# h's parts laid out by pairs of k over four token blocks, in a hybrid attention and MLP block

## The chip, the cores and the metric

The kernel runs on one core of a Trainium2 chip. The metric is the device time of one execution in microseconds. A comparison is made on medians of several runs; the profile beside it is of one execution.

## What is computed

One decoder layer on a sequence of 1024 tokens with a width of 1024, in float32. The part that the change touches is the first third: a normalized and modulated input h, and one projection of it to 2304 columns, from which two kinds of attention take their heads. The rest is the output projection and an MLP of width 4096 with squared ReLU.

```
h = rms_norm(x, g_attn_pre) * (1 + sc_a) + sh_a
proj = h @ w_in                                   # 1024 x 2304
oa = banded_attention(...)                        # window of 128, with sinks
ob = dilated_mixture_attention(...)               # three dilated windows
mixed = concat([rms_norm(oa, g_mix_a), rms_norm(ob, g_mix_b)])
x = x + gt_a * rms_norm(mixed @ w_out, g_attn_post)
h = rms_norm(x, g_mlp_pre) * (1 + sc_m) + sh_m
x = x + gt_m * rms_norm(square(relu(h @ w_up)) @ w_down, g_mlp_post)
```

## The kernel before

**Numbers in two parts.** Every matmul operand is split into an upper part, a float32 rounded to the format that TensorE takes (fp32r), and a lower part, the rest. One product is three matmuls: upper by upper, lower by upper, upper by lower. ACT writes an upper part with a copy, DVE or POOL the lower one with a subtraction.

**Where h lies.** The tile `hw` has 128 partitions, 8 slots, 2 parts and 1024 floats (line 422). Tokens are counted in eight blocks of 128, the width of h in eight pieces k of 128 (the contraction). Before, slot t holds token block t; inside it piece k stands at 128k. `mod_chunk` (lines 677 to 695) fills it from `xnT`, the transposed normalized input: for one k, ACT writes the upper part (line 689), then h itself in place (line 686), and DVE the lower part (line 692). For k 0 and 1 it does so in two halves of four token blocks, for the others over all eight at once.

**The projection.** There are six units u (two of them for the banded attention, four for the dilated one), each of three column tiles c of 128 and two token halves x of 512. A tile (u, x, c) adds eight products, one for each k, in one bank of PSUM. `proj_mm` (lines 859 to 869) emits the three matmuls (lines 866, 867 and 869): the stationary operand is the weight, the moving one is h of the half x, read as four blocks of 128 tokens out of four slots. The first unit goes through `first_unit` (tile name `acc`), the others through `proj_tile` (tile name `pj`), whose products are the "dense" work of PE that stands between the steps of attention.

**The order of the work.** The program is written out by a planner, the class `Sched`. It holds a queue of steps for every engine, each with a planned duration, what it waits for, and resources that it takes and gives (`Res`). It emits whichever step can start first by its own clock, so planned durations and the moments at which resources come free decide the order of the instructions on each engine. Each engine then works through its instructions in that order; real waits are those of the data and of the tiles. A planned release that has no tile behind it is no wait on the chip.

**Where h's place goes next.** `hw` is used again. When the projection is nearly done, `load_wo` (lines 1339 to 1365) brings in `w_out` in eight parts k: a DMA to a staging tile (line 1348), a multiplication by a column of gains on ACT into `hw[:, k, 0]` (line 1353), and the lower part into `hw[:, k, 1]` by DVE (line 1356) or by POOL in two instructions (lines 1361 and 1362), whichever the planner finds free. Each part takes one unit of the resource `r_wo`; it is given by `proj_tile` in the last column tile (u 5, c 2): four units after the last k of x 0, four after the last k of x 1. `load_wo` is opened when at most two projection tiles are still to be emitted. `open_out` (lines 1367 to 1381) opens the output projection when the dense work is done, the last tile of the projection has been handed on, and all eight parts of `w_out` have been planned. It loads a gate (line 1377); then `out_block` takes one token block after another: it loads the attention output (line 1423), splits it (lines 1436 and 1439) and multiplies it with the parts in `hw` (lines 1478 to 1480, tile name `y_ps`).

**Attention.** A step of it has scores on PE (lines 1127 and 1182), a maximum on DVE (1146), exponentials on ACT (1153), the normalization on POOL (1158), transposes on PE (1232 to 1239), the split of the result on ACT and DVE (1246 and 1250) and the product with the values on PE (1262 to 1274).

**The MLP** fills the rest of the time, with seven products of quarters for each of its eight halves (lines 1902 to 1904).

Of the kernel before, what the change touches and what calls it, by code (L numbers as in the profile page):

```python
# [10 lines left out]
F32 = mybir.dt.float32  # L11
# [4 lines left out]
ALU = mybir.AluOpType  # L16
# [3 lines left out]
P = 128  # L20
D = 1024
S = 1024
KC = D // P
# [151 lines left out]
class Sched:  # L175
# [20 lines left out]
    def op(self, eng, dur, emit, deps=(), **kw):  # L196

        o = self.step(dur, emit, deps, **kw)
        o.alts = None
        if isinstance(eng, str):  # L200
            self.queue[eng].append(o)
        else:
            o.alts = dict(zip(eng, zip(dur, emit)))
            for e in eng:
                self.queue[e].append(o)
        return o.ev
# [113 lines left out]
def t_sb(n):  # L320
    return 0.098 + 0.00083 * n
# [6 lines left out]
def t_dv(n):  # L328
    return 0.066 + 0.00104 * n
# [19 lines left out]
def hybrid_block(ctx: ExitStack, tc: tile.TileContext, x, positions, w_ada, b_ada, g_attn_post, w_in, w_out,  # L349
# [3 lines left out]
    V, A, G, T = nc.vector, nc.scalar, nc.gpsimd, nc.tensor  # L353
    x, out = x[0], out[0]
    w_ada, w_out, w_up, w_down = w_ada[0], w_out[0], w_up[0], w_down[0]
    sc = Sched()
    op, pe_op = sc.op, sc.pe_op

    def pool(name, bufs=1, side="left", space=None, stack=ctx):
        kw = dict(name=name, bufs=bufs, reuse_waits="tile")  # L360
        if space is not None:
            kw["space"] = space
        else:
            kw["side"] = side
        return stack.enter_context(tc.tile_pool(**kw))
# [20 lines left out]
    r_u, r_raw, r_h2, r_wo = Res(0), Res(0), Res(0), Res(0)  # L386
# [35 lines left out]
    hw = pool("hw", 1).tile([P, KC, 2, 1024], F32R, name="hw")  # L422
# [45 lines left out]
    xnT = p0.tile([P, KC, S], F32, name="xnT")  # L468
# [56 lines left out]
    w_raw, w_rawe, w_hl, w_e = {}, {}, {}, {}  # L525
# [45 lines left out]
    e = op("ACT", 0.1, lambda: A.activation(cond[:], c_raw, AF.Exp, scale=-1.0), [e_c], prio=0)  # L571
# [32 lines left out]
    e = op("DVE", 4.2, f_turns, [e_pos, e_c], prio=1)  # L604
# [34 lines left out]
    def mod_group(g):  # L639
# [30 lines left out]
        for half in ((0, 1) if g == 0 else (None,)):  # L670
            for k in range(2 * g, 2 * g + 2):
                mod_chunk(k, eg, half)
# [4 lines left out]
    def mod_chunk(k, eg, half):  # L677
        t0, t1 = (0, TB) if half is None else (4 * half, 4 * half + 4)
        n = (t1 - t0) * P
        ks = slice(k * P, (k + 1) * P)  # L680
        h, hh = xnT[:, k, t0 * P:t1 * P].rearrange("p (b t) -> p b t", t=P), hw[:, t0:t1, 0, ks]
        deps = [eg] + (e_xn[0] + e_xn[1] if half is None else e_xn[half])

        def full(eng):
            if eng is A:
                return lambda: A.activation(h, h, AF.Identity, bias=s_a[:, k:k + 1], scale=g_a[:, k:k + 1])
            return lambda: V.tensor_scalar(h, h, g_a[:, k:k + 1], s_a[:, k:k + 1], ALU.mult, ALU.add)

        eh = op("ACT", t_sb(n) + 2 * AP_COST, lambda: A.activation(hh, h, AF.Identity, bias=s_a[:, k:k + 1],
                                                                  scale=g_a[:, k:k + 1]), deps, prio=0)  # L690
        e = op("ACT", t_sb(n) + 2 * AP_COST, full(A), [eh], prio=0)
        e = op("DVE", t_dv(n), lambda: V.tensor_tensor(hw[:, t0:t1, 1, ks], h, hh.bitcast(F32), ALU.subtract), [e],
               prio=0)
        for x in (0, 1) if half is None else (half,):
            e_hh[k, x], e_hl[k, x] = eh, e
# [39 lines left out]
    qs, ks, vs, e_q, e_k, n_in = {}, {}, {}, {}, {}, {}  # L735
# [117 lines left out]
    def dense(dur, emit, deps, **kw):  # L853
        return pe_op("dense", dur, emit, deps, **kw)

    def w_at(u, c, k):
        return divmod(3 * k + c, 4) if u == 0 else (2 * c + k // 4, k % 4)

    def proj_mm(ps, u, c, k, x, part):
        i, n = w_at(u, c, k)  # L860
        t, w = slice(k * P, (k + 1) * P), w_hl[u, i]
        n = slice(n * P, n * P + P)
        h = [hw[:, 4 * x:4 * x + 4, i, t] for i in range(2)]
        ps = ps[:].rearrange("p (b t) -> p b t", t=P)
        if part != 1:
            T.matmul(ps, w[:, 0, n], h[0], start=(k == 0), stop=False)  # L866
            T.matmul(ps, w[:, 1, n], h[0], start=False, stop=False)  # L867
        if part != 0:
            T.matmul(ps, w[:, 0, n], h[1], start=False, stop=(k == KC - 1))  # L869
# [18 lines left out]
    def first_unit():  # L888
        order = [(k, part, x, c) for x in range(2) for k in range(2) for part in range(2) for c in range(3)]
        order += [(k, part, x, c) for k in range(2, AHEAD) for part in range(2) for x in range(2) for c in range(3)]  # L890
        order += [(k, part, x, c) for x in range(2) for c in range(3) for k in range(AHEAD, KC) for part in range(2)]
        last = {w_at(0, c, k)[0]: i for i, (k, _, _, c) in enumerate(order)}
        accs[FILL] = acc_at[FILL][0].tile([P, 512], F32, name="acc", tag=acc_at[FILL][1])
        acc_at[FILL][2].free.pop()
        for i, (k, part, x, c) in enumerate(order):
            a = 3 * x + c
            pl, tag, r = acc_at[a]
            first = k == 0 and part == 0 and a != FILL

            def emit(k=k, part=part, x=x, c=c, a=a, pl=pl, tag=tag, first=first):  # L900
                if first:
                    accs[a] = pl.tile([P, 512], F32, name="acc", tag=tag)
                fill.open |= a == FILL
                proj_mm(accs[a], 0, c, k, x, part)

            def after(k=k, part=part):
                if part:
                    tick()
                if k == KC - 1:
                    sc.filler = None  # L910
            d = dense(0.454 if part == 0 else 0.227, emit,
                      [w_e[0, w_at(0, c, k)[0]], (e_hl if part else e_hh)[k, x]] + (e_xn[0] + e_xn[1] if a == 5 else []),
                      takes=[(r, 1)] if first else [], after=after, gives=[(r_w, 1)] if last[w_at(0, c, k)[0]] == i else [])
            if k == KC - 1 and part:
                yield (0, x, c, lambda a=a: accs[a], d, r)
# [4 lines left out]
    def proj_tile(u, x, c):  # L920
        b = []
        for k in range(KC):
            def emit(k=k):
                if k == 0:
                    b.append(pj.tile([P, 512], F32, name="pj", tag="pj"))
                proj_mm(b[0], u, c, k, x, None)
            gives = []
            if x and k % 4 == 3:
                gives.append((r_w, 1))
            if u == 5 and c == 2 and k == KC - 1:  # L930
                gives.append((r_wo, 4))
            d = dense(0.681, emit, [w_e[u, w_at(u, c, k)[0]]], takes=[(r_pj, 1)] if k == 0 else [], gives=gives, after=tick)
        evac(u, x, c, lambda: b[0], d, r_pj)

# [11 lines left out]
    def feed_proj():  # L946
        if len(sc.pe.get("dense", [])) <= 4 and todo_dense:
            u, x, c = todo_dense.pop(0)
            if (x, c) == (1, 0):
                next_unit_w(u)  # L950
            if (u, x, c) == (2, 0, 0):
                for e_ in e_tab:
                    e_.clear()
                tables([(0, 1, 4)], lambda i: stage("rows")[:].rearrange("p (b r) -> p b r", b=TB), r_stg, r_x,
                       lambda: px.tile([P, 4, P], F32, name="ptab", tag="x"), [[e_rot[1, 0]], [e_rot[1, 1]]])
            proj_tile(u, x, c)
        return not todo_dense
# [1122 lines left out]
```

## Time and profile before

| | |
|---|---|
| median of 3 runs | 1147.73 us (1147.73 to 1148.61) |
| the profiled execution, its own time | 1148.87 us |
| its span, first to last instruction | 1147.1 us |
| mean granted TensorE clock | 0.992 of full speed |
| projection among attention ends, first output matmul | 377.55 us, 398.38 us from the span's start |
| matmuls | 5417 |

How to read what follows: times in rows are microseconds from the start of the span, unless marked ns. PE is TensorE with its matmuls, PEld its weight loads, DVE is VectorE, ACT is ScalarE, POOL is GpSimd, SP issues the DMAs. A row of the timeline has start, duration, engine, line of the kernel, operation, output and inputs, count, and in brackets the idle time ahead of it with what ended it. A row of the groups has line, engine, operation, shapes and count, then the busy time and the mean duration of one in ns, then idle time ahead. A matmul's recorded duration runs from its entry to the end of its output, so two that follow each other closely overlap in the record.

### The profile page before, as it was taken

What the parts mean: (1) busy time and instruction counts of PE and PEld (TensorE: products, weight loads), DVE (VectorE), ACT (ScalarE), POOL (GpSimd) and SP (SyncE); (2) the same over time, 40 slices, a digit from 0 to 9 for tenths busy, and PEclk for the clock granted to TensorE, in tenths of its full rate; (3) what the DMA queues carried; (4) which work ended last, traced back from release to release, by engine and by line L of the source; (5) the groups of instructions that cost most, each with busy time, mean ns of one, the idle gap of its engine ahead of it and who ended that gap; (6) DMA issues with size and microseconds to landing.
All of it is one profiled execution on the core that took longest, in us unless ns stands there. A gap on an engine that the chain in (4) does not pass through costs nothing.

```text
span 1147.1 us, 15609 instructions
## 1 busy us (share of the span) xinstructions
PE 1115.2 (97%) x5417; PEld 924.1 (81%) x5417; DVE 818.7 (71%) x1380; ACT 635.9 (55%) x1101; POOL 265.7 (23%) x349
## 2 busy tenths in 40 slices
PE   8999999999999899998999999999999999999996
PEld 7788878888888687887788888888888888888885
DVE  7878666666667765668979664599644896537998
ACT  8868865464556756675675424563234733246542
POOL 2458867565743521111000000000000000000002
PEclk9999999999999899998999999999999999999999
DMA  9556454343423305552981168812469112584103
GB/s 347 192 204 164 163 158 164 136 155 127 146 71 132 124 26 186 203 207 104 352 306 39 41 224 285 303 37 74 147 230 332 70 56 76 201 307 168 37 19 147
DMA packets 90910, 185.29 MB, mean 162 GB/s; under 512 B 8400, under 2 KB 31056, under 8 KB 90832
## 3 DMA queue, kind: packets, MB, share of 16 engines
q1 hardware_dynamic: 90832, 184.30, 46.3%
q8 instruction: 43, 0.70, 0.2%
q14 instruction: 35, 0.29, 0.1%
HBM read 137.08 MB, written 28.31 MB: 144 GB/s over the span
## 4 chain that ended last, share of the span: by engine, by line
PE 76%; DVE 8%; issue 4%; ACT 4%; POOL 4%; DMA 3%; SPq 1%; DVEq 0%; POOLq 0%; ACTq 0%
PE mlp_ps L1903 16%; PE mlp_ps L1904 16%; PE mlp_ps L1902 16%; PE pj L866 3%; PE pj L869 3%; PE pj L867 3%; PE s_ps L1127 3%; PE o_ps L1262 2%; PE pt_ps L1232 1%; PE y_ps L1478 1%; PE y_ps L1480 1%; PE y_ps L1479 1%; PE pt_ps L1235 1%; DVE hw L1673 1%; PE o_ps L1267 1%
## 5 line engine op out<-in xcount | busy, mean ns | idle before, releaser
L1902 PE MATMUL mlp_ps<-hw 128*128 128x512 f32 x896 | 350.7, 391 | 0.4 <-ACT hw L1664 0.4
L1903 PE MATMUL mlp_ps<-hw 128*128 128x512 f32 x896 | 349.5, 390 | 1.1 <-DVE hw L1670 1.1
L1904 PE MATMUL mlp_ps<-hw 128*128 128x512 f32 x896 | 349.4, 390 | 0.0
L1903 PEld LDWEIGHTS mlp_ps<-hw 128*128 128x128 f32 x896 | 168.7, 188 | 36.9 <-DVE hw L1670 1.4
L1902 PEld LDWEIGHTS mlp_ps<-hw 128*128 128x128 f32 x896 | 168.8, 188 | 36.4 <-ACT hw L1664 0.8
L1904 PEld LDWEIGHTS mlp_ps<-hw 128*128 128x128 f32 x896 | 168.6, 188 | 35.0
L1673 DVE TENSOR_TENSOR hw<-w,hw 128x1024 fp32r<-128x1024 f32 x96 | 114.7, 1221 | 95.1 <-ACT hw L1666 93.0
L1666 ACT CAST hw<-w 128x1024 fp32r<-128x1024 f32 x96 | 97.5, 1047 | 129.8 <-PE mlp_ps L1904 93.1
L2002 POOL TENSOR_TENSOR st<-st,nhalf 128x1 f32<-128x1 f32 x8 | 7.8, 977 | 604.1 <-DVE st L2000 604.1
L866 PE MATMUL pj<-hw,w_hl 128*128 128x512 f32 x240 | 102.5, 427 | 0.0
L869 PE MATMUL pj<-hw,w_hl 128*128 128x512 f32 x240 | 94.6, 394 | 0.0
L867 PE MATMUL pj<-hw,w_hl 128*128 128x512 f32 x240 | 94.5, 394 | 0.0
L1250 DVE TENSOR_TENSOR ph<-pt_ps,ph 128x512 fp32r<-128x512 f32 (+1 forms) x110 | 69.5, 648 | 34.6 <-ACT ph L1246 34.3
L1666 ACT CAST hw<-u 128x1024 fp32r<-128x1024 f32 x48 | 48.7, 1051 | 64.6 <-PE mlp_ps L1904 64.6
L1246 ACT CAST ph<-pt_ps 128x512 fp32r<-128x512 f32 (+1 forms) x110 | 58.9, 555 | 32.9 <-PE pt_ps L1235 27.5
L1153 ACT ACTIVATE p_sb<-p_sb,mn 128x128 f32<-128x128 f32 (+3 forms) x64 | 49.8, 778 | 38.3 <-DVE mn L1146 36.8
L1673 DVE TENSOR_TENSOR hw<-u,hw 128x1024 fp32r<-128x1024 f32 x48 | 57.1, 1220 | 18.2 <-ACT hw L1666 18.2
L1960 DVE TENSOR_TENSOR yacc<-yacc,mlp_ps 128x512 f32<-128x512 f32 x96 | 62.2, 683 | 3.3 <-PE mlp_ps L1904 3.3
L1158 POOL TENSOR_SCALAR p_sb<-p_sb,den 128x128 f32<-128x128 f32 (+3 forms) x64 | 48.4, 762 | 53.1 <-DVE den L1156 51.9
L1015 POOL TENSOR_TENSOR ada_acc<-ada_acc,wa_st 128x512 f32<-128x512 f32 x42 | 55.3, 1318 | 3.5
L869 PEld LDWEIGHTS pj<-hw,w_hl 128*128 128x128 f32 x240 | 45.1, 188 | 10.5
L1478 PE MATMUL y_ps<-hw,oh 128*128 128x512 f32 x128 | 51.7, 404 | 0.0
(206 smaller groups left out, 2010.4 us busy)
## 6 DMA issues: line engine op xcount, KB each, us to landing
hw<-s_dram SPq DMA_DIRECT2D x84, 512.0 KB, 4.4
wa_st<-in_w_ada SPq DMA_DIRECT2D x32, 512.0 KB, 4.4
w<-in_w_up SPq DMA_DIRECT2D x32, 512.0 KB, 4.8
w<-in_w_down SPq DMA_DIRECT2D x32, 512.0 KB, 7.5
s_dram<-hw SPq DMA_DIRECT2D x28, 512.0 KB, 4.3
qt<-hl SPq DMA_DIRECT2D x40, 256.0 KB, 2.8
w_st<-in_w_in SPq DMA_DIRECT2D x36, 256.0 KB, 3.1
x_sb<-in_x SPq DMA_DIRECT2D x16, 512.0 KB, 6.1
```

The lines of the kernel that those rows point to most:

```text
L866: T.matmul(ps, w[:, 0, n], h[0], start=(k == 0), stop=False)
L867: T.matmul(ps, w[:, 1, n], h[0], start=False, stop=False)
L869: T.matmul(ps, w[:, 0, n], h[1], start=False, stop=(k == KC - 1))
L1246: A.copy(b["ph"][:, 0, :w], b["pt"][:, :w])
L1250: V.tensor_tensor(b["ph"][:, 1, :w], b["pt"][:, :w], b["ph"][:, 0, :w].bitcast(F32), ALU.subtract)
L1478: T.matmul(ps[:], b["oh"][:, k], wh[:, c0:c0 + 512], start=(k == 4 * m), stop=False)
L1666: A.copy(out[j][0], flat(src[j]))
L1673: V.tensor_tensor(out[j][1], flat(src[j]), out[j][0].bitcast(F32), ALU.subtract)
L1902: T.matmul(ps[m][:], sh, mh, start=starts and k == 0, stop=False, **kw)
L1903: T.matmul(ps[m][:], sh, ml_, start=False, stop=False, **kw)
L1904: T.matmul(ps[m][:], sl, mh, start=False, stop=k == 3, **kw)
L1960: e = op("DVE", t_dv(512), lambda: V.tensor_tensor(y(), y(), ps[m][:], ALU.add), [e, ml.e_y[tb, n]], gives=gives, prio=1)
```

## The change

The eight slots of `hw` are numbered anew. Slot 4x + j holds, for the token half x, the pieces k = 2j and 2j + 1, each as one run of 512 tokens. `mod_chunk` writes its two parts there: one run of 512 for a half, two runs for all tokens. `proj_mm` reads one run of 512, and hands PSUM's bank to the matmul without a view in four blocks. Since a slot is now read by two k only, `proj_tile` gives one unit of `r_wo` after each odd k of the last column tile instead of four after the last k. Instructions, their number and their planned durations stay as they are.

```diff
     def mod_chunk(k, eg, half):
         t0, t1 = (0, TB) if half is None else (4 * half, 4 * half + 4)
         n = (t1 - t0) * P
-        ks = slice(k * P, (k + 1) * P)
-        h, hh = xnT[:, k, t0 * P:t1 * P].rearrange("p (b t) -> p b t", t=P), hw[:, t0:t1, 0, ks]
+        h = xnT[:, k, t0 * P:t1 * P].rearrange("p (x t) -> p x t", t=512)
+        hh, hl = (hw[:, t0 // 4 * 4 + k // 2:t1 - 3 + k // 2:4, i, k % 2 * 512:k % 2 * 512 + 512] for i in range(2))
...
-        e = op("DVE", t_dv(n), lambda: V.tensor_tensor(hw[:, t0:t1, 1, ks], h, hh.bitcast(F32), ALU.subtract), [e],
+        e = op("DVE", t_dv(n), lambda: V.tensor_tensor(hl, h, hh.bitcast(F32), ALU.subtract), [e],
                prio=0)
...
     def proj_mm(ps, u, c, k, x, part):
         i, n = w_at(u, c, k)
-        t, w = slice(k * P, (k + 1) * P), w_hl[u, i]
-        n = slice(n * P, n * P + P)
-        h = [hw[:, 4 * x:4 * x + 4, i, t] for i in range(2)]
-        ps = ps[:].rearrange("p (b t) -> p b t", t=P)
+        w, n = w_hl[u, i], slice(n * P, n * P + P)
+        h = [hw[:, 4 * x + k // 2, i, k % 2 * 512:k % 2 * 512 + 512] for i in range(2)]
+        ps = ps[:]
...
-            if u == 5 and c == 2 and k == KC - 1:
-                gives.append((r_wo, 4))
+            if u == 5 and c == 2 and k % 2:
+                gives.append((r_wo, 1))
```

## The prediction

> **What bounds the kernel now.** I read the page's first rows (who is busy), then the table by stage, then the timelines around the one place where the change lets something start earlier.
>
> ```profile
> PE 1115.2 (97%) x5417; PEld 924.1 (81%) x5417; DVE 818.7 (71%) x1380; ACT 635.9 (55%) x1101; POOL 265.7 (23%) x349
> ```
>
> ```profile
> 68.00:377.00 309.00, 304.26 (x1721) 256.03 (x1720) 209.14 (x566) 189.45 (x454) 194.13 (x254) 1.00 0.46 150
> 377.00:398.00 21.00, 15.92 (x92) 12.86 (x91) 17.62 (x48) 17.77 (x35) 12.92 (x11) 0.91 0.32 111
> ```
>
> The second fence is the windows view: window, its length, then busy us of PE, weight loads, DVE, ACT, POOL, then granted clock, DMA share, GB/s. TensorE (PE) is the bound: 304.26 of 309 us while projection and attention share it. Only 377 to 398, after the last projection matmul and before the first of the output projection, has PE at 15.92 of 21: **5.08 us idle**, while DVE (17.62) and ACT (17.77) are nearly full. So the change can pay in two ways: cheaper projection matmuls where PE is full, or a better filled hole at 377.
>
> **The matmuls.** Before, a projection matmul's moving operand is four runs of 128 floats, 8 KB apart; after, one run of 512. The trace of before has both kinds. In the groups by line and shape (count, then busy us, mean ns):
>
> ```profile
> L866 PE MATMUL pj<-hw,w_hl 128*128 128x512 f32 x240 | 102.5, 427 | 0.0
> L867 PE MATMUL pj<-hw,w_hl 128*128 128x512 f32 x240 | 94.5, 394 | 0.0
> L867 PE MATMUL acc<-hw,w_hl 128*128 128x512 f32 x48 | 18.8, 391 | 0.0
> L1479 PE MATMUL y_ps<-hw,oh 128*128 128x512 f32 x128 | 50.4, 394 | 0.0
> L1478 PE MATMUL y_ps<-hw,oh 128*128 128x512 f32 x128 | 51.7, 404 | 0.0
> L1903 PE MATMUL mlp_ps<-hw 128*128 128x512 f32 x896 | 349.5, 390 | 1.1 <-DVE hw L1670 1.1
> ```
>
> L1479, L1478 and L1903 read one run of 512; L866 and L867 read four. L867 takes 394 ns among attention matmuls, exactly what the one-run L1479 takes there, and 391 in the first unit, where little is mixed in, against 390 in the MLP. L866's 427 is that of the first matmul of a group of three, recorded as it enters behind other work (L1478, also first, shows 404 against 394). So the runs cost nothing that these rows show: **0 us** taken. The far end: all 720 `pj` matmuls at the MLP's 390 would be 240 x 37 ns + 480 x 4 ns = 10.8 us less. On the other side even 404 for all gives 720 x 0.404 = 290.9 against 240 x 0.427 + 480 x 0.394 = 291.6: no loss.
>
> **The writes of h.** ACT writes the upper part (L689) and DVE the lower (L692) in eight runs of 128 before, two of 512 after; a half-width call goes from four runs to one.
>
> ```profile
> L689 ACT ACTIVATE hw<-xnT,s_a,g_a 128x1024 fp32r<-128x1024 f32 x6 | 7.1, 1235 | 2.3 <-DVE s_a L668 2.3
> L686 ACT ACTIVATE xnT<-xnT,s_a,g_a 128x1024 f32<-128x1024 f32 x6 | 7.1, 1232 | 0.0
> L692 DVE TENSOR_TENSOR hw<-xnT,hw 128x1024 fp32r<-128x1024 f32 x6 | 7.1, 1221 | 3.0 <-ACT xnT L686 3.0
> L1673 DVE TENSOR_TENSOR hw<-w,hw 128x1024 fp32r<-128x1024 f32 x96 | 114.7, 1221 | 95.1 <-ACT hw L1666 93.0
> ```
>
> L686 does L689's arithmetic into one run: 3 ns less. L1673, the same subtraction in one run, takes 1221 like L692. Ends: 6 x 3 ns gained, nothing lost; taken as 0. Count and planned cost of these instructions stay, so the planner's order stays until the changed `gives` is reached.
>
> **The earlier release.** `hw` is also the place of the output weights: part k of `w_out` goes into slot k. Before, the planner may load parts 0 to 3 after the last k of tile (u 5, x 0, c 2) and parts 4 to 7 after the last k of (5, 1, 2), since every k read every slot of its half. After, slot 4x+k//2 is read by two k alone, and one part is released at each odd k. Nothing is added: no instruction, DMA or wait; eight loads on SP, eight multiplications on ACT and eight lower parts (five on DVE, three as pairs on POOL) move up in their queues. For x 0, PE is full until the projection ends (304.26 of 309 above), so I cost that half at nothing; the cover is the projection, and without it the price would be the 2.18 us that two multiplications hold ACT. For x 1 the L869 of k = 1, 3, 5, 7:
>
> ```profile
> 369.79 0.40 PE L869 MATMUL pj<-hw,w_hl 128*128 128x512 f32 x1
> 372.54 0.39 PE L869 MATMUL pj<-hw,w_hl 128*128 128x512 f32 x1
> 374.83 0.40 PE L869 MATMUL pj<-hw,w_hl 128*128 128x512 f32 x1
> 377.15 0.40 PE L869 MATMUL pj<-hw,w_hl 128*128 128x512 f32 x1
> ```
>
> Four gives at 377.55 become one each at 370.2, 372.9, 375.2 and 377.55: 7.4, 4.6, 2.3 and 0 us earlier, and the later loads no longer queue behind three others. What follows on SP, ACT, DVE and POOL in before:
>
> ```profile
> 372.12 2.03 SPq L1348 DMA_DIRECT2D wo_st<-in_w_out  x4
> ...
> 391.82 0.33 SPq L1377 DMA_DIRECT2D gate_a<-gate_d  x1
> 392.26 0.38 SPq L1423 DMA_DIRECT2D o_sb<-o_dram  x1
> ```
>
> ```profile
> DMA to landing us min/median/max: 4.3/5.1/6.4
> ```
>
> ```profile
> 376.88 0.59 ACT L1246 CAST ph<-pt_ps 128x512 fp32r<-128x512 f32 x1 [2.81 <-PE pt_ps L1235]
> ...
> 384.35 1.16 ACT L1353 ACTIVATE hw<-wo_st,head 128x1024 fp32r<-128x1024 f32 x1
> ...
> 387.82 2.19 ACT L1353 ACTIVATE hw<-wo_st,head 128x1024 fp32r<-128x1024 f32 x2
> ...
> 396.68 1.05 ACT L1436 CAST oh<-o_sb 128x1024 fp32r<-128x1024 f32 x1 [0.73 <-DMA o_sb<-o_dram]
> ```
>
> ```profile
> 384.48 0.69 DVE L847 TENSOR_TENSOR v_hl<-pv,v_hl 128x512 fp32r<-128x512 f32 x1 [0.45 <-ACT v_hl L844]
> ...
> 389.31 2.49 DVE L1356 SCALAR_TENSOR_TENSOR hw<-wo_st,head,hw 128x1024 fp32r<-128x1024 f32 x1
> ```
>
> ```profile
> 380.26 0.59 POOL L1158 TENSOR_SCALAR p_sb<-p_sb,den 128x384 f32<-128x384 f32 x1 [5.79 <-DVE den L1156]
> ...
> 392.86 2.40 POOL L1362 TENSOR_TENSOR hw<-wo_st,hw 128x1024 fp32r<-128x1024 f32 x1
> 395.22 2.47 POOL L1158 TENSOR_SCALAR p_sb<-p_sb,den 128x640 f32<-128x640 f32 x3
> ```
>
> The reader is to see a chain: the last lower part on DVE ends at 391.80; at 391.82 SP issues the gate and then the attention output for block 0 (the output stage opens only when all eight parts are planned); that lands for ACT at 396.68, and PE starts L1478 at 398.38 (last row below). The loads themselves were issued at 372.12 already, since the release is the planner's alone: the chip has the data from about 372.12 + 4.3 = 376.4 on, yet ACT has the multiplications behind attention work until 384.35 to 390.0. After, the first two can run at about 376.5 to 379. That takes two of four, 2.2 us of ACT, out of the stretch where ACT, DVE and POOL hold attention up, and lets POOL (idle 5.79 us before 380.26) do its share before 387 instead of holding the normalizations until 395.22.
>
> ```profile
> 392.78 0.39 PE L1262 MATMUL o_ps<-ph,v_hl 128*128 128x256 f32 x1 [1.33 <-DVE ph L1250]
> ...
> 396.09 0.48 PE L1232 MATMUL pt_ps<-head,p_sb 128*128 128x128 f32 x1 [0.16 <-POOL p_sb L1158]
> 396.97 0.48 PE L1232 MATMUL pt_ps<-head,p_sb 128*128 128x128 f32 x1 [0.40 <-POOL p_sb L1158]
> ...
> 398.38 0.78 PE L1478 MATMUL y_ps<-hw,oh 128*128 128x512 f32 x1
> ```
>
> How early can L1478 come? The next condition is that the last projection is posted, after L847 at 385.17: at most 6.6 us earlier; I take about 4, so near 394.5. An earlier start is worth only the idle PE time it fills: after 394.5 the 0.16 + 0.40 above. The relief of ACT I count at its 2.2 us, PE idling behind those engines. Sum **2.8 us** of the 5.08. The ends: 0, if attention's own chain (PE to ACT to DVE, the 1.33 above) keeps its length, and 5.08, if the hole closes. Past 398 PE is the bound again, so I let the gain last to the end. The profiled execution took 1148.87 (1147.1 of it span), 1.14 above the median of 1147.73, against which the prediction is made: 1147.73 - 2.8 = **1144.9**.
>
> **The rivals.** *The clock keeps up.* Windows of 4 us, same columns:
>
> ```profile
> 380.00:384.00 4.00, 2.79 (x22) 2.23 (x20) 3.38 (x14) 3.88 (x11) 1.65 (x3) 1.00 0.06 16
> 384.00:388.00 4.00, 2.85 (x20) 2.27 (x18) 3.49 (x8) 3.95 (x7) 1.75 (x3) 1.00 0.06 16
> 388.00:392.00 4.00, 2.85 (x19) 2.08 (x17) 4.00 (x7) 3.95 (x7) 3.92 (x3) 1.00 0.09 20
> 392.00:396.00 4.00, 2.93 (x13) 2.37 (x13) 3.33 (x14) 2.53 (x6) 3.92 (x4) 0.80 0.78 250
> 396.00:400.00 4.00, 3.50 (x12) 2.88 (x13) 2.86 (x8) 3.29 (x6) 2.47 (x4) 0.50 0.16 47
> 400.00:404.00 4.00, 4.00 (x27) 3.62 (x26) 2.58 (x6) 1.73 (x3) 0.29 (x2) 0.85 0.00 0
> ```
>
> After 12 us with PE at 71% (8.49 of 12) the granted clock falls to half; 0.20, 0.50 and 0.15 of 4 us each make 3.4 us lost. If PE is fuller before 394, this may not happen: 1144.9 - 3.4 = 1141.5. Against it: the first part of the hole remains, and where the clock decides is not seen. The Trainium skill ("TensorE: Matmul & The Clock Gate", Part 1: The HAM clock gate) has the half rate come back after an idle window of some 3.4 us; by that rule short gaps would not cost the clock, and a fuller PE would change nothing here. The trace disagrees: the longest gap ahead of the fall that the rows show is 1.33 us, and the clock fell.
>
> *Nothing moves.* The matmuls cost the same and attention's own chain sets the hole; 1147.7.
>
> *The four runs do cost.* 427 against 390 is theirs: 1147.73 - 10.8 = 1136.9. L867 at 394 beside the one-run L1479 at 394 speaks against it.
>
> *Slower: a multiplication ahead of its data.* ACT works in order. The planner expects a load within some 3.4 us (its own costs); after the give at 370.2 it may put the first multiplication before the CAST of 376.88. The load issued at 372.12 lands after 5.1 us (median), 6.4 at most: 377.2 to 378.5. Then ACT stands until there, 0.3 to 1.6 us, and so may the next one. The projection that would cover it ends at 377.55, so PE idles as long. Two waits at the far end, 3.2 us: 1150.9. It decides from the point where the first multiplication stands ahead of that CAST and its load lands later than 376.9. For it: the landing times. Against it: ACT idled 2.81 us there anyway.
>
> **How the numbers follow.** Chances: forecast 0.42 (its own range 1142.7 to 1147.7, from 5.08 to 0 gained), clock 0.20, nothing 0.15, four runs 0.04, slower 0.19. A measurement of this kernel tells about 0.2%, 2.3 us, from no change, so faster means below 1145.4. Of the forecast 0.25 lies there; with clock and four runs: faster 0.49. The rest of it, nothing, and a little of slower: same 0.33; slower 0.18. Leaving out the far side of the four runs and the tails of both signs, the range is 1139.5 to 1151.0.
>
> **What would show it.** Right: L867 and L869 stay at 394 and 391; L689 and L692 within 10 ns; the first L1353 of the second half near 377 instead of 384; L1377 and L1478 about 4 us earlier; the stage between last projection and first output matmul with less than 5 us idle; everything up to about 340 us as before. Wrong: matmul means that fall by over 3 ns; L1353 early but PE waiting as long for DVE and POOL; an ACT wait on `wo_st` followed by idle PE; a gain at 398 that is gone by 520.

## The result, and the profile after

The changed kernel is slower: 1150.62 us (median of 17 runs, 1148.62 to 1153.84) against 1147.99 (17 runs, 1146.44 to 1151.07) for the kernel before. The ratio is **1.0025 [1.0017, 1.0032]**, some 2.6 us. (A ratio with an interval is not the quotient of the two medians; it differs from that by up to 0.0007 below.) The forecast was 2.8 us the other way. The execution that was profiled took 1149.36 us, 1.26 below its own median, while that of before lay 0.88 above its median. So the two traces differ by only 0.49 us in total. They show where time moved; how much it is worth is read from the medians.

The line numbers of the kernel after are one lower than those of before from line 863 on: L866, L867 and L869 are now L865, L866 and L868, L1353 and L1356 are L1352 and L1355, L1361 and L1362 are L1360 and L1361, and L1478 is L1477.

First the parts costed at nothing. From the page of after, its busiest engines and two groups:

```profile
PE 1113.5 (97%) x5417; PEld 923.0 (80%) x5417; DVE 821.9 (72%) x1381; ACT 636.0 (55%) x1101; POOL 263.7 (23%) x347
...
L865 PE MATMUL pj<-hw,w_hl 128*128 128x512 f32 x240 | 102.4, 427 | 0.0
L866 PE MATMUL pj<-hw,w_hl 128*128 128x512 f32 x240 | 94.5, 394 | 0.0
```

And from its groups by line and shape, the writes of h:

```profile
L689 ACT ACTIVATE hw<-xnT,s_a,g_a 128x1024 fp32r<-128x1024 f32 x6 | 7.1, 1236 | 2.3 <-DVE s_a L668 2.3
...
L692 DVE TENSOR_TENSOR hw<-xnT,hw 128x1024 fp32r<-128x1024 f32 x6 | 7.1, 1221 | 3.0 <-ACT xnT L686 3.0
```

One run of 512 takes 427 and 394 ns where four runs of 128 took 427 and 394; the writes take 1236 and 1221 against 1235 and 1221. By these rows the layout itself does nothing. The only other difference on the first page is that DVE has one instruction more and POOL two less: one lower part of `w_out` went from POOL to DVE.

The windows of the stage 342 to 378 (start and end, length, then busy us of PE, weight loads, DVE, ACT, POOL, then granted clock, DMA share, GB/s) show a loss where the prediction had counted on a full PE. Before:

```profile
342.00:378.00 36.00, 35.91 (x211) 30.61 (x210) 24.31 (x58) 21.61 (x43) 12.40 (x12) 1.00 0.42 153
```

After:

```profile
342.00:378.00 36.00, 34.30 (x202) 29.11 (x201) 24.77 (x57) 20.68 (x42) 11.52 (x12) 1.00 0.38 138
```

PE loses 1.61 us, with projection products still queued. The timeline of after around 355 says how (start, duration, engine, line, operation, tiles; in brackets the idle time ahead and what ended it):

```profile
352.92 2.40 POOL L1361 TENSOR_TENSOR hw<-wo_st,hw 128x1024 fp32r<-128x1024 f32 x1
...
352.68 0.59 ACT L1245 CAST ph<-pt_ps 128x512 fp32r<-128x512 f32 x1
...
353.22 3.18 DVE L1355 SCALAR_TENSOR_TENSOR hw<-wo_st,head,hw 128x1024 fp32r<-128x1024 f32 x1
356.33 0.68 DVE L1249 TENSOR_TENSOR ph<-pt_ps,ph 128x512 fp32r<-128x512 f32 x1
...
357.06 0.38 PE L1261 MATMUL o_ps<-ph,v_hl 128*128 128x256 f32 x1 [1.40 <-DVE ph L1249]
357.52 0.40 PE L865 MATMUL pj<-hw,w_hl 128*128 128x512 f32 x1
378.79 0.40 PE L868 MATMUL pj<-hw,w_hl 128*128 128x512 f32 x1
```

The reader is to see a chain over four engines. POOL subtracts one lower part of `w_out` from 352.92 to 355.32. DVE starts another at 353.22, which takes 3.18 us and ends at 356.40, 1.08 after POOL's. Behind it in DVE's queue waits attention's split L1249, whose input from ACT was ready at 353.27. It starts at 356.33. The product L1261 waits for it, PE stands for 1.40 us, and the projection products that would fill the gap stand *behind* L1261 in PE's queue. Another 0.30 us of idle PE lies at 348.69 (the row stands below, with e9). The last `pj` matmul starts at 378.79 instead of 377.15. Most of that arises here: from the 636th of the 720 `pj` matmuls, which starts just before 342 in both traces, to the last one it is 36.93 us, against 35.44 before.

In the hole after the projection the same thing comes again, and the chain towards the output stage is longer, not shorter. The matmul L836 that stands 2.28 us here stood 0.41 in before. Timeline of after:

```profile
381.78 2.38 POOL L1361 TENSOR_TENSOR hw<-wo_st,hw 128x1024 fp32r<-128x1024 f32 x1
...
383.27 1.98 DVE L1355 SCALAR_TENSOR_TENSOR hw<-wo_st,head,hw 128x1024 fp32r<-128x1024 f32 x1 [0.56 <-ACT hw L1352]
...
385.63 0.66 PE L836 MATMUL pv<-head,vt 128*128 128x128 f32 x4 [2.28 <-DVE ot L1297]
...
386.20 0.52 SPq L1376 DMA_DIRECT2D gate_a<-gate_d  x1
388.79 3.25 SPq L1300 DMA_DIRECT2D o_dram<-ot  x2
393.57 0.38 SPq L1422 DMA_DIRECT2D o_sb<-o_dram  x1
...
400.76 1.04 ACT L1435 CAST oh<-o_sb 128x1024 fp32r<-128x1024 f32 x1
...
402.80 0.48 PE L1477 MATMUL y_ps<-hw,oh 128*128 128x512 f32 x1
```

The gate L1376 is issued at 386.20, 5.6 us earlier than before. But the attention output of the first block (L1422) comes at 393.57, 1.3 us later than before, behind the stores L1300 of 388.79 on SP's queue. ACT then takes it up only at 400.76, behind attention's work, 7.2 us after its issue where before had it after 4.4. So the first output product comes at 402.80, 4.4 us later.

Why the two profiled executions end nearly together: windows of 4 us near 532, first of before, then of after.

```profile
528.00:532.00 4.00, 0.94 (x5) 0.52 (x4) 2.00 (x2) 1.57 (x3) 2.40 (x1) 0.86 0.00 0
532.00:536.00 4.00, 4.00 (x15) 3.42 (x14) 3.21 (x9) 3.38 (x5) 0.00 (x0) 0.50 0.00 0
536.00:540.00 4.00, 4.00 (x16) 3.21 (x15) 2.75 (x5) 2.10 (x3) 0.00 (x0) 0.78 0.00 0
```

```profile
532.00:536.00 4.00, 2.63 (x11) 2.44 (x12) 1.65 (x6) 3.83 (x5) 0.14 (x1) 0.70 0.00 0
536.00:540.00 4.00, 4.00 (x17) 3.25 (x16) 3.60 (x8) 2.94 (x5) 0.00 (x0) 0.87 0.00 0
```

Before loses 0.14 + 0.50 + 0.22 of 4 us, 3.4 us, after 0.30 + 0.13, 1.7 us. The output products of after end 1.73 us later than those of before (their last one starts at 516.80 against 515.07). From there to the end of the last matmul before takes 622.17 us and after 620.93, so in these two executions the clock gives back most of that. It falls differently from one execution to the next.

### The profile page after: what moved, and what is told of

Read it like the earlier page. It is cut to its first block, busy times and chain, and to the rows that moved or that the text cites. A ratio compares the mean times of both kernels' runs of the same rounds, so it can differ in the third digit from the quotient of the medians.

```text
span 1147.3 us, 15607 instructions
## 1 busy us (share of the span) xinstructions
PE 1113.5 (97%) x5417; PEld 923.0 (80%) x5417; DVE 821.9 (72%) x1381; ACT 636.0 (55%) x1101; POOL 263.7 (23%) x347
## 4 chain that ended last, share of the span: by engine, by line
PE 72%; DVE 9%; DMA 6%; issue 4%; ACT 4%; POOL 4%; SPq 1%; DVEq 0%; POOLq 0%; ACTq 0%
PE mlp_ps L1902 16%; PE mlp_ps L1903 16%; PE mlp_ps L1901 16%; PE pj L865 3%; PE pj L868 3%; PE pj L866 3%; PE s_ps L1126 3%; DMA wa<-in_w_ada 2%; PE o_ps L1261 2%; PE pt_ps L1231 1%; DMA x_sb<-in_x 1%; DVE hw L1672 1%; DMA wo_st<-in_w_out 1%; POOL ada_acc L1014 1%; PE pt_ps L1234 1%
## 5 line engine op out<-in xcount | busy, mean ns | idle before, releaser
L865 PE MATMUL pj<-hw,w_hl 128*128 128x512 f32 x240 | 102.4, 427 | 0.0
L868 PE MATMUL pj<-hw,w_hl 128*128 128x512 f32 x240 | 94.6, 394 | 0.0
L866 PE MATMUL pj<-hw,w_hl 128*128 128x512 f32 x240 | 94.5, 394 | 0.0
L1249 DVE TENSOR_TENSOR ph<-pt_ps,ph 128x512 fp32r<-128x512 f32 (+1 forms) x110 | 69.4, 648 | 26.9 <-ACT ph L1245 26.5
L1672 DVE TENSOR_TENSOR hw<-u,hw 128x1024 fp32r<-128x1024 f32 x48 | 57.1, 1221 | 18.2 <-ACT hw L1665 18.2
L1157 POOL TENSOR_SCALAR p_sb<-p_sb,den 128x128 f32<-128x128 f32 (+3 forms) x64 | 50.9, 799 | 49.7 <-DVE den L1155 44.3
L868 PEld LDWEIGHTS pj<-hw,w_hl 128*128 128x128 f32 x240 | 45.1, 188 | 10.4
L1477 PE MATMUL y_ps<-hw,oh 128*128 128x512 f32 x128 | 51.1, 399 | 0.0
```

Source lines behind the costliest of these rows:

```text
L1249: V.tensor_tensor(b["ph"][:, 1, :w], b["pt"][:, :w], b["ph"][:, 0, :w].bitcast(F32), ALU.subtract)
L1672: V.tensor_tensor(out[j][1], flat(src[j]), out[j][0].bitcast(F32), ALU.subtract)
```

## The experiments

Two theories stood after this. **The meeting:** a lower part on DVE that overlaps one on POOL is held, attention's split is queued behind it, and PE, in order, stands. **The wait:** the multiplication on ACT (now L1352) stands ahead of its load, ACT's later work is late, and with it everything else. The trace of after has both: besides the rows above, ACT waits 2.48 us at 346.15 and 1.87 us at 377.56 for `wo_st`.

### The layout alone, and each half of the release alone

e1_layout_only: the new layout with before's release.

```diff
-            if u == 5 and c == 2 and k % 2:
-                gives.append((r_wo, 1))
+            if u == 5 and c == 2 and k == KC - 1:
+                gives.append((r_wo, 4))
```

> The new layout with the old release (four units after the last k). Release theory (the loss comes from where the eight parts of w_out now stand in the queues, the layout is free): as before, ratio 0.999 to 1.001, last pj matmul at 377.2 +- 0.3, first y_ps matmul near 398.4. Layout theory (the one-run operand, the writes or the waits on a slot cost the time): ratio about 1.0025 and pj matmuls or stages longer before 340 us.

e2_early_x0: the early release for x 0 alone.

```diff
-            if u == 5 and c == 2 and k % 2:
-                gives.append((r_wo, 1))
+            if u == 5 and c == 2 and (k == KC - 1 if x else k % 2):
+                gives.append((r_wo, 4 if x else 1))
```

> New layout, one unit per pair of k for x 0 alone; x 1 gives four at its end as before. Release theory: the PE gap near 357 us stays, the last pj matmul at about 378.8 (+1.6 us against before), and since PE is the bound behind it most of the loss is here: ratio 1.0012 to 1.0025. If the loss sits in the second half (x 1, the 2.28 us PE gap at 383 and the later first y_ps matmul): ratio 1.000, pj ends at 377.2.

e3_early_x1: the early release for x 1 alone.

```diff
-            if u == 5 and c == 2 and k % 2:
-                gives.append((r_wo, 1))
+            if u == 5 and c == 2 and (k % 2 if x else k == KC - 1):
+                gives.append((r_wo, 1 if x else 4))
```

> New layout, one unit per pair of k for x 1 alone; x 0 gives four at its end. If the loss is in the first half: ratio 0.998 to 1.001 and the last pj matmul at 377.2. If the second half loses: ratio 1.0012 to 1.0025, with a first y_ps matmul later than 398.4. What the prediction hoped for (the hole after 377 closes by 2.8 us) would give 0.9975.

Measured, beside 1148.13 for before: e1 1148.66, ratio 0.9998 [0.9985, 1.0010]; e2 1150.88, 1.0030 [1.0020, 1.0040]; e3 1150.05, 1.0012 [1.0000, 1.0024]. No cost of the layout shows, so the loss comes from the release. The half of x 0, which was to cost nothing, costs about as much as the whole change; the half of x 1 gains nothing. The two losses do not add up to that of the whole change, and why is open. Both ratios lie above what was expected of them (1.0012 to 1.0025, and 0.998 to 1.001).

One expectation of e1 failed: its last `pj` matmul starts at 378.94, not near 377.2. It is 1.8 us late already at 342, for a reason that stays open; after, with the same layout, is 0.16 us late there. From the 636th `pj` matmul to the last it takes 35.43 us, as before does (35.44). So a point in time can't be compared between two traces, only the length of a stage: 36.93 in after, 37.28 in e2, 35.42 in e3.

In e2, the same stage and the same rows (windows, then timeline):

```profile
342.00:378.00 36.00, 33.95 (x199) 28.86 (x197) 24.76 (x57) 19.75 (x41) 11.45 (x12) 1.00 0.37 130
```

```profile
346.04 1.15 ACT L1352 ACTIVATE hw<-wo_st,head 128x1024 fp32r<-128x1024 f32 x1 [2.84 <-DMA wo_st<-in_w_out]
...
348.59 0.66 PE L836 MATMUL pv<-head,vt 128*128 128x128 f32 x4 [0.67 <-ACT vt L830]
...
353.12 3.16 DVE L1355 SCALAR_TENSOR_TENSOR hw<-wo_st,head,hw 128x1024 fp32r<-128x1024 f32 x1
...
356.93 0.39 PE L1261 MATMUL o_ps<-ph,v_hl 128*128 128x256 f32 x1 [1.38 <-DVE ph L1249]
```

PE loses 35.91 - 33.95 = 1.96 us there: 1.38 behind DVE's split, and 0.67 behind ACT's copy L830 at 348.59, just after ACT had stood 2.84 us for a load. In e3 the stage up to 378 keeps its 35.90. What it does right after is in its timeline:

```profile
374.83 1.15 ACT L1352 ACTIVATE hw<-wo_st,head 128x1024 fp32r<-128x1024 f32 x1 [0.86 <-DMA wo_st<-in_w_out]
377.45 1.15 ACT L1352 ACTIVATE hw<-wo_st,head 128x1024 fp32r<-128x1024 f32 x1 [1.47 <-DMA wo_st<-in_w_out]
...
379.13 0.38 PE L1261 MATMUL o_ps<-ph,v_hl 128*128 128x256 f32 x1 [0.51 <-ACT ph L1245]
380.58 0.39 PE L1261 MATMUL o_ps<-ph,v_hl 128*128 128x256 f32 x1 [1.07 <-DVE ph L1249]
```

Two multiplications do come before 380, as forecast, but the second waits 1.47 us for its load with the splits behind it, and PE, whose projection has just ended, idles 0.51 + 1.07 us. Here the wait is real and uncovered.

### The lower parts on DVE alone

e4_lower_on_dve is the kernel after with no lower part on POOL.

```diff
-            ph2.e_wo[k] = op(("DVE", "POOL"), (t_dv(D) + AP_DV, t_pts(D) + t_ptt(D)), (f_lo, f_lo2), [eh],
+            ph2.e_wo[k] = op("DVE", t_dv(D) + AP_DV, f_lo, [eh],
                              gives=[(r_stg, 1)], prio=4)
```

> The changed kernel with all eight lower parts of w_out on DVE, none on POOL. Overlap theory (a lower part on DVE that overlaps one on POOL takes 2 to 3.2 us instead of 1.28 and holds the next split of attention behind it): every L1355 at 1.3 us, the PE gap of 1.40 us at 357 gone, ratio against before 1.000 or less. Order theory (ACT and DVE lose the time of the parts wherever they stand ahead of attention's splits, overlap or not): PE gaps of 1 to 2 us remain between 346 and 362, ratio 1.001 to 1.003.

e5_before_dve makes the same edit in the kernel before.

> The kernel before (old layout, old release) with all lower parts of w_out on DVE. If overlap of DVE and POOL is what those parts cost wherever they stand: also faster than before, ratio 0.996 to 0.999, DVE L1356 at 1.3 us throughout, since before too has overlaps (2.49 and 1.80 us). If DVE alone pays only together with the early release: 0.9995 to 1.002 here, and the early release is worth something on its own once POOL is out of it.

e4: 1145.25, ratio to before 0.9977 [0.9969, 0.9986]. e5: 1144.78 beside 1147.74, ratio 0.9970 [0.9959, 0.9981], the lowest of the study, though the intervals of the two overlap. Without lower parts on POOL the early release shows no worth either way. In e4 ACT waits as long as in after, and yet DVE's lower part keeps its own length, and the product that stood at 357 has no gap (timeline of e4):

```profile
348.14 1.15 ACT L1352 ACTIVATE hw<-wo_st,head 128x1024 fp32r<-128x1024 f32 x1 [2.42 <-DMA wo_st<-in_w_out]
...
355.21 1.27 DVE L1355 SCALAR_TENSOR_TENSOR hw<-wo_st,head,hw 128x1024 fp32r<-128x1024 f32 x1
```

And e5 speaks against any worth of an early output stage (timeline of e5):

```profile
397.42 0.53 SPq L1377 DMA_DIRECT2D gate_a<-gate_d  x1
398.04 0.40 SPq L1423 DMA_DIRECT2D o_sb<-o_dram  x1
...
405.81 0.39 PE L1478 MATMUL y_ps<-hw,oh 128*128 128x512 f32 x1
...
513.14 0.39 PE L1480 MATMUL y_ps<-hw,ol 128*128 128x512 f32 x1
```

Its first output product comes 7.4 us later than in before (405.81 against 398.38), its last one 1.9 us earlier (513.14 against 515.07). This trace has no fall of the clock in the hole, though, where that of before loses 3.4 us; e10 below makes the same comparison without this difference.

### A planner that expects the loads later, or takes the parts in turn

e6_late_plan: in the kernel after, the planner counts 1.5 us more for each load of `w_out`, so that the multiplications are placed later.

```diff
-            end = self.dma + 0.8
+            end = self.dma + (2.3 if o.kind == "wo" else 0.8)
```

> The changed kernel, with the planner told that a load of w_out lands 1.5 us later than it assumed, so that no multiplication is put in ACT's queue ahead of its data. If ACT's waits for these loads (2.48 and 1.87 us in the changed kernel) are the price: waits under 0.5 us and ratio 1.000. If the overlap of lower parts is: ratio stays 1.001 to 1.003, with a DVE L1355 over 2 us followed by a PE gap over 1 us.

e7_in_turn: a lower part is planned only after the one before it, so that two are not meant to run beside each other.

```diff
-            ph2.e_wo[k] = op(("DVE", "POOL"), (t_dv(D) + AP_DV, t_pts(D) + t_ptt(D)), (f_lo, f_lo2), [eh],
+            ph2.e_wo[k] = op(("DVE", "POOL"), (t_dv(D) + AP_DV, t_pts(D) + t_ptt(D)), (f_lo, f_lo2), [eh] + ([ph2.e_wo[k - 1]] if k else []),
```

> The changed kernel, POOL allowed, but the planner starts a lower part only after the lower part before it. Overlap theory: DVE L1355 at 1.3 us, the gap near 357 gone, ratio 1.000 or less. If POOL is dear by its own length (3.5 us before the normalizations) and not by overlap: still 1.001 to 1.003.

e8_dve_late_plan: the edits of e4 and e6 together.

> All lower parts on DVE and the later landing in the plan, both on the changed kernel. If ACT's waits cost on top of the overlap: below e4_lower_on_dve, 0.995 to 0.997. If they are covered by PE's other work: the same as e4_lower_on_dve within 0.001, that is 0.997 to 0.999.

Beside 1147.74: e6 1146.19, 0.9981 [0.9968, 0.9993]; e7 1146.86, 0.9989 [0.9979, 1.0000]; e8 1145.40, 0.9983 [0.9973, 0.9994]. By itself e6 speaks for the wait: without a wait of ACT in this stage the loss is gone. But it moves the meeting too, and makes it cheaper. Timeline of e6:

```profile
347.77 1.15 ACT L1352 ACTIVATE hw<-wo_st,head 128x1024 fp32r<-128x1024 f32 x1
...
354.45 2.23 DVE L1355 SCALAR_TENSOR_TENSOR hw<-wo_st,head,hw 128x1024 fp32r<-128x1024 f32 x1 [0.74 <-ACT hw L1352]
...
357.34 0.39 PE L1261 MATMUL o_ps<-ph,v_hl 128*128 128x256 f32 x1 [0.49 <-DVE ph L1249]
```

DVE enters later, is held for less, and PE stands 0.49 instead of 1.40 us. e7 keeps both the wait and a meeting:

```profile
346.26 1.15 ACT L1352 ACTIVATE hw<-wo_st,head 128x1024 fp32r<-128x1024 f32 x1 [2.38 <-DMA wo_st<-in_w_out]
...
354.49 2.01 DVE L1355 SCALAR_TENSOR_TENSOR hw<-wo_st,head,hw 128x1024 fp32r<-128x1024 f32 x1
```

It has no gap at 357, since the split that PE needed ran at 353.41, ahead of the lower part. So it is not the meeting as such that costs, but what stands behind it. e8 adds nothing to e4. None of the three tells the theories apart cleanly; the next one does so for x 0.

### The decisive one, and the same question in the kernel before

e9_x0_dve: e2, with the lower parts of k 0 to 3 on DVE alone. The release, the loads and the multiplications stay early.

```diff
-            ph2.e_wo[k] = op(("DVE", "POOL"), (t_dv(D) + AP_DV, t_pts(D) + t_ptt(D)), (f_lo, f_lo2), [eh],
-                             gives=[(r_stg, 1)], prio=4)
+            ph2.e_wo[k] = (op("DVE", t_dv(D) + AP_DV, f_lo, [eh], gives=[(r_stg, 1)], prio=4) if k < 4 else
+                           op(("DVE", "POOL"), (t_dv(D) + AP_DV, t_pts(D) + t_ptt(D)), (f_lo, f_lo2), [eh], gives=[(r_stg, 1)], prio=4))
```

> As e2_early_x0 (early release for x 0 alone, ratio 1.0030), but the first four lower parts on DVE alone. Overlap theory: the whole loss of e2 hangs on one DVE lower part that stands behind POOL's (3.16 us instead of 1.28), so the gap of 1.38 us near 357 goes and the ratio falls to 0.999 to 1.001. If the early multiplications on ACT (ahead of their data by 2.84 us) are the price: 1.002 to 1.004 as in e2.

e10_before_hole_dve and e11_before_first_dve: the kernel before with the same choice for k 4 to 7 (`if k > 3`) and for k 0 to 3.

> The kernel before, with the last four lower parts (the hole after 377 us) on DVE alone; the first four free to go to POOL as before. If the gain of e5_before_dve (0.997) is made in the hole, where DVE stood behind POOL for 2.49 us and POOL held the normalizations until 395: 0.996 to 0.9985. If it is made before 377: 1.000.

> The kernel before, with the first four lower parts on DVE alone, the last four free. PE is full there before, so if the hole makes the gain of e5_before_dve: 0.999 to 1.001. If the parts before 377 make it: 0.996 to 0.9985.

e12_lower_on_pool: the kernel after with all eight lower parts on POOL.

```diff
-            ph2.e_wo[k] = op(("DVE", "POOL"), (t_dv(D) + AP_DV, t_pts(D) + t_ptt(D)), (f_lo, f_lo2), [eh],
+            ph2.e_wo[k] = op("POOL", t_pts(D) + t_ptt(D), f_lo2, [eh],
```

> The changed kernel with all eight lower parts on POOL, none on DVE. If it is the meeting of two lower parts that costs: no DVE instruction with two SBUF operands meets them so often, ratio 0.998 to 1.001. If POOL's own length costs (3.5 us each in front of the normalizations, and the gate of the output stage behind the last one): slower than the changed kernel, over 1.003.

Beside 1147.79: e9 1148.42, 1.0003 [0.9994, 1.0012]; e10 1146.06, 0.9986 [0.9978, 0.9995]; e11 1147.80, 0.9998 [0.9988, 1.0007]; e12 1150.40, 1.0022 [1.0012, 1.0033]. In e9 the loss of e2 is gone, and the wait is still there (timeline of e9):

```profile
345.65 1.15 ACT L1352 ACTIVATE hw<-wo_st,head 128x1024 fp32r<-128x1024 f32 x1 [2.24 <-DMA wo_st<-in_w_out]
...
352.72 1.27 DVE L1355 SCALAR_TENSOR_TENSOR hw<-wo_st,head,hw 128x1024 fp32r<-128x1024 f32 x1
```

Its PE is busy 35.93 of the 36 us from 342 to 378, and from the 636th `pj` matmul to the last it takes 34.94 us, against 37.28 in e2. So for x 0 most of the price is the meeting. The wait has a price of its own once it is longer than what PE has queued. Timeline of after, then of e4:

```profile
348.69 0.66 PE L836 MATMUL pv<-head,vt 128*128 128x128 f32 x4 [0.30 <-ACT vt L830]
```

```profile
350.69 0.66 PE L836 MATMUL pv<-head,vt 128*128 128x128 f32 x4 [0.24 <-ACT vt L830]
```

ACT's copy L830 stands behind the multiplication that waited. After waits of 2.05 (e12) and 2.24 us (e9) no such gap of PE is listed; it is 0.19 after 2.38 (e7), 0.24 after 2.42 (e4), 0.30 after 2.48 (after) and 0.67 after 2.84 (e2): the wait less some 2.2 us.

The kernel before has a meeting too, in the hole, which the prediction looked at without seeing it: the DVE row at 389.31 with 2.49 us. Its POOL rows (timeline of before):

```profile
388.32 2.39 POOL L1362 TENSOR_TENSOR hw<-wo_st,hw 128x1024 fp32r<-128x1024 f32 x1
390.69 2.09 POOL L1361 TENSOR_SCALAR wo_st<-wo_st,head 128x1024 f32<-128x1024 f32 x1
```

DVE's row ends at 391.80, 1.09 us after POOL's subtraction at 390.71. e10 takes POOL out of the hole alone (timeline of e10):

```profile
390.06 1.28 DVE L1356 SCALAR_TENSOR_TENSOR hw<-wo_st,head,hw 128x1024 fp32r<-128x1024 f32 x1
...
392.54 0.39 PE L1262 MATMUL o_ps<-ph,v_hl 128*128 128x256 f32 x1 [0.34 <-DVE ph L1250]
```

PE's gap there falls from 1.33 to 0.34 us and the kernel is faster by 0.14%. The clock of the two traces falls alike, by 3.4 us from 394 on. From the last `pj` matmul to the last output product e10 takes 136.93 us against 137.92, 0.99 less, as much as the gap lost. Its first output product comes at 406.76, 8.4 us later than before's, so an early output stage was worth nothing here. e11, which does it where before had no costly meeting, changes nothing.

e12 has no lower part of `w_out` on DVE, and it is slow all the same, between the two outcomes that were named for it. POOL needs two instructions, some 3.5 us, for what DVE does in 1.28. And the meeting is still there, with another DVE instruction that reads two operands from SBUF, the lower part of a rotated head (timeline of e12):

```profile
360.44 2.40 POOL L1361 TENSOR_TENSOR hw<-wo_st,hw 128x1024 fp32r<-128x1024 f32 x1
...
361.34 2.05 DVE L771 TENSOR_TENSOR hl<-hl 128x512 fp32r<-128x512 f32 x1
...
364.58 0.39 PE L1261 MATMUL o_ps<-ph,v_hl 128*128 128x256 f32 x1 [1.16 <-DVE ph L1249]
```

L771 takes 0.69 us on DVE at 152.38 in the same trace. Here it takes 2.05, attention's split comes after it, and PE stands 1.16 us. How much of e12's loss is POOL's length and how much this meeting isn't separated. DVE alone is the better place, not merely one engine alone.

**What the clock has in it.** Every run lists its mean granted clock, to three digits. The means over the runs: 0.9929 for after (17 runs); 0.9931, 0.9935 and 0.9939 for before in the three groups of runs (35, 30 and 31 of them); 0.9923 for e2 and 0.9945 for e3, beside 0.9931; 0.9955 for e4 beside 0.9931; 0.9958 for e5, 0.9948 for e6 and e7 and 0.9947 for e8 beside 0.9935; 0.9929 for e9, 0.9945 for e10, 0.9928 for e11 and 0.9924 for e12 beside 0.9939. Of 1148 us, 0.001 is 1.15 us. So the estimate is that e4 and e5 lose 2.8 and 2.6 us less to the clock, against 2.9 and 3.0 us between the medians, and e2 0.9 us more, of 2.75. These are upper estimates. What a fall costs can be read from the end of the last output product to the end of the last matmul, where no part of the change lies. That stretch takes 620.05 to 620.11 us in the three traces without a fall near its start (e3, e4, e5), 620.61 to 620.95 in the nine with one of 1.7 us, and 622.17 in the two with one of 3.4 (before, e7). So a third to three fifths of a fall show in the time. By this the clock would have about 0.9 to 1.6 of e5's 3.0 us, an estimate from these stretches. e9 and e12 lose at most 1.1 and 1.7 us more to the clock than before. e3 loses some 1.5 us less to the clock and is still 1.9 us slower by its median, so its work has become longer.

## Why the prediction was wrong

**Matmuls and writes: right.** 0 us for the runs of the moving operand and for the writes of h; the rows agree to 1 ns, and e1 is 0.9998 [0.9985, 1.0010]. With them the rival "the four runs do cost" falls.

**The step that failed** is "PE is full until the projection ends, so I cost that half at nothing; the cover is the projection". A PE that is full in the profile of before covers a delay only as far as the products *ahead* of the waiting one reach. PE takes its matmuls in order, and the planner puts attention's products between the projection's. One late split on DVE therefore stops PE with projection work queued behind it: 1.40 us at 357 in after, 1.38 in e2, nothing in e9. The price that I gave for an absent cover, the 2.18 us of two multiplications on ACT, was near in size and on the wrong engine: DVE's lower part was what came late.

**Under it lay a second error:** a lower part was costed by the engine it ran on, as if POOL's share were independent of DVE's. The row at 389.31, 2.49 us against the 1.28 of a lone one in e10, stood quoted in the prediction. I read it as work, and it was a hold.

**The x 1 half:** the whole forecast gain of 2.8 us was to come from it, and e3 measures 1.0012 [1.0000, 1.0024]. Multiplications came near 377 and the gate 5.6 us earlier, both as forecast. But the "relief of ACT" came back as waits for loads, 1.47 us with PE idle 0.51 + 1.07 (e3), and in after as the meeting of 383.27 with PE idle 2.28 us. "An earlier start is worth only the idle PE time it fills" was right, but L1477 did not come 4 us earlier: it came 4.4 us later in after, its input behind the stores of attention on SP and then behind attention on ACT, and 0.5 us earlier in e3 (397.91). In e10 a start 8.4 us later goes with a faster kernel. For this half the traces place the loss, but no run takes the waits or the meeting out of it alone.

**The rivals.** "A multiplication ahead of its data" happened as described, with ACT standing 2.48 and 1.87 us in after. It had a price where it was placed, at the end of the projection (x 1); in x 0, where I had not looked for it, it has 0.30 of the 1.70 us that PE stands in after, and 0.67 of 2.05 in e2. So the direction was this rival's, and its mechanism is the smaller part of the cause there. "The clock keeps up" did not come true for after (0.9929). The traces of e4 and e5 have no fall in the hole, but that a fuller hole keeps the clock up isn't shown: e1 has none either, with a gap of 1.32 us where before has 1.33, and e10 has before's full fall with e5's gap of 0.34.

**Open:** e2 loses 2.75 us by its median, of which the trace places 1.96 in PE's stage before 378; the rest is in part the clock, and isn't itemised. The gain of e5 is separated only as far as single traces go: 0.99 us for the shorter chain by e10, which has e5's gap there and before's fall, and by estimate 0.9 to 1.6 for the clock, of 3.0 us in all. No run holds the clock fixed. The early release with the old layout wasn't tried, as it would let `w_out` overwrite parts of h still to be read.

## What to carry to other kernels

A busy engine hides a delay only with what stands ahead of the waiting instruction in its own queue; before costing a moved step at nothing, look at what is queued behind it on each engine that it touches. A planner that offers a step to two engines must know whether they can work side by side: here, giving the step to the one quick engine (e5, 0.9970 [0.9959, 0.9981]) had the lowest ratio, though e6, which keeps the choice and moves the steps, overlaps it (0.9981 [0.9968, 0.9993]). And a row that is longer than its equals is to be asked what ran beside it before it is moved.

## What the runs showed of the hardware

**DVE and POOL exclude each other in these instructions.** A lower part on DVE, which reads two operands from SBUF, takes 1.27 to 1.29 us alone, and 3.18, 3.16, 2.49, 2.23, 2.01 or 1.98 beside POOL's subtraction, ending 1.08 or 1.09 us after it in each of these. It is not a matter of two lower parts of `w_out`: the one at 360.72 in before takes 1.80 beside a normalization on POOL (L1158 at 360.54, 0.91 us), and L771 in e12 takes 2.05 instead of 0.69. It goes the other way too: POOL's multiplication at 390.69 in before, entered while DVE's lower part ran, took 2.09 us where a lone one takes 1.13. The Trainium skill ("SBUF — State Buffer", Who interferes with whom) says that a DVE instruction with two SBUF inputs contends with a GpSimd instruction that reads SBUF, and that the shared ports are an exclusive lock. The rows agree: DVE's instruction is not slowed a little but ends a little less than its own length after POOL's end.

**Four runs of 128 floats, 8 KB apart, stream into TensorE as fast as one of 512:** 394 against 394 ns over 240 matmuls.

**The clock's falls vary between executions.** The mean granted clock of after's 17 runs lies between 0.990 and 0.996. In the profiled executions a fall halves the clock for 3.4 or 6.8 us, which takes away 1.7 or 3.4 us, most often near 390, 442 or 533. e4 and e5 have none at these places, e1, e6 and e8 none near 390, and e3 none near 533.
